# Mixer B's third score product: 128 rows instead of 64

## The chip, the cores and the metric

The kernel runs on one core of a Trainium2 chip. The metric is the device time of one execution in microseconds, the median of several. TensorE multiplies and transposes, VectorE and ScalarE work on tiles in SBUF and PSUM, GpSimd on tiles in SBUF; each takes its instructions in order. TensorE is written PE in the profile, its weight loads PEld, VectorE DVE, ScalarE ACT, GpSimd POOL, SyncE SP.

## The reference

One inference step of four layers over 640 tokens (512 sample tokens, 128 prompt tokens) of 1024 features. Each layer is a token mixer and an MLP with squared ReLU; the mixers go A, B, C, A. All arithmetic is float32. The change concerns mixer B, the second layer, a latent attention with 16 heads:

```python
q = (rmsnorm(h @ w_dq, g_q) @ w_uq).reshape(b, t, N_HEADS, NOPE_DIM + ROPE_DIM)   # 64 + 32
kv = (c_kv @ w_ukv).reshape(b, t, N_HEADS, NOPE_DIM + V_DIM)
k = jnp.concatenate([k_nope, broadcast(k_rope)], axis=-1)      # k_rope: one for all heads
p = softmax(q @ k^T * 96 ** -0.5);  o = p @ v
```

Sample rows see 128 context keys and the 512 sample keys, 640 in all; prompt rows see the 128 prompt keys. So a head has scores of 512 x 640 and of 128 x 128.

## The kernel before

**Two parts.** TensorE gets its operands in the type fp32r, which carries fewer bits than float32. So each operand is split into a high part (ScalarE copies it and rounds) and a low part (VectorE subtracts), and a product is made as high x high + low x high + high x low. In mixer B a query block has 128 rows: the 64 features of the head as high parts and, in the other 64 rows, as low parts. For an even head the high parts are in rows 0 to 63, for an odd one in rows 64 to 127.

**Keys of a pair.** Heads are taken by pairs (class PairB). `nk` (line 729) makes both heads' keys in PSUM, rows 0 to 63 the first head's, rows 64 to 127 the second's, in two parts of 384 columns (t = 0, 1). `ka` (741) copies head e's rows into a tile `kt[e]` of its own as high parts, `kc` (750) copies them again into that tile's other 64 rows, and `kb` (754) writes the low parts into the third tile, `kt[2]`, which both heads share: each has 64 rows of it.

**Scores.** `Kern.qk` (1019) makes a score block with three products: the query block with the doubled high keys (128 rows: high x high and low x high), the rotary query block `R` with `Kr` (128 rows), and the query block's 64 rows of high parts with the low keys (64 rows). `Pair.qk` (407) calls it for a block of 128 sample queries twice, once for each 320 of the 640 keys; `zq` (534) calls it for both heads' prompt queries with 256 columns, the second 128 of which are used. The scores lie in two PSUM tiles of two banks, named psl; `mx` (427, VectorE) copies them out negated with the least value, `ex` (ScalarE) takes exponentials, `sc` (449, GpSimd) scales. Then TensorE transposes the probabilities (`tr`: ps<-cst,p), ScalarE and VectorE split them (ar<-ps) and TensorE multiplies with the values (ps<-ar,VS). Transpositions, projections and keys share three PSUM banks (`tb`).

**Tiles.** High and low parts of weights and keys lie in twelve tiles named wa, each 128 x 1024, a queue: `walloc` (887) takes from its front, `wfree` appends. Twelve are there in all (line 821). The key tiles are given back when the pair's nine score steps are made (`done`, 772); a weight's two tiles when its last product is made.

**Order.** `attend` (1077) goes through the list PLAN["B"] once for each of 8 pairs and their lags; each entry is a step of a pair ("ka00.2": key step of part 0, head 0, of the pair that began two rounds before). The steps' calls are made in exactly this order, so each engine's queue follows it. In a round, eight score steps (64 over the eight pairs) and one prompt step of a pair stand among other steps; behind the last of them come the next pair's projections: `nq`, `nk` on TensorE, `nh`, `ka`, `kc` on ScalarE, `nl`, `kb` on VectorE. Beside the fifth pair and after it, part of the output projection runs too. All engine calls of recorded stages are made at line 283, hence "L283" in the profile.

Of the kernel before, what the change touches and what calls it, by code (L numbers as in the profile page):

```python
# [21 lines left out]
T = 640  # L22
# [22 lines left out]
# the order of the recorded calls of each phase  # L45
# [167 lines left out]
# the steps of two heads (Pair) in the order of a round, each with the rounds that it lags behind its pair's first  # L213
# [33 lines left out]
class Engine:  # L247
    """an engine whose calls go through Calls"""
# [8 lines left out]
class Calls:  # L257
    """the core; between keep and replay the engines' calls are kept, to be made in an order of their own"""
# [26 lines left out]
    def cut(self):  # L285
        """what follows on the tensor engine is no part of the group of products before it"""
        self.apart = True
# [17 lines left out]
class Stream:  # L305
    """Weight units in the order of their use: loaded, and split into two parts that fp32r carries exactly."""
# [44 lines left out]
    def open(self):  # L351
        """past a None, at which fill stops"""
        self.n += 1
# [11 lines left out]
class Pair:  # L365
    """Two heads' attention in steps named as in PLAN: a method and the head, block or group that it takes.

    Sample rows: scores (qk), negated copy and its least value (mx; sk puts the sink beside it), exponentials with
    their sums (ex), inverse sums (rc), scaling (sc), by key blocks transposition (tr), its two parts (hi, lo) and the
    product with the values (pv), at last the output's two parts (oh, ol). The z steps do the same for the prompt rows.  # L370
    """
# [17 lines left out]
    @property  # L389
    def st(self):  # L390
        """[-max | sum | 1/sum] of eight row blocks and the two of the prompt"""
        if self.st_ is None:
            self.st_ = self.k.sts()
        return self.st_
# [28 lines left out]
    def x(self, e, b, sink=0):  # L423
        """the row block's probabilities (sink = 1: with the sink's, which lies before them)"""
        return self.X[e, b // 2][:, b % 2, 1 - sink:1 + A_WIN[b][1]] if self.A else self.X[e, b]
# [78 lines left out]
    def pa(self, e):  # L504
        """stacked products: the values' low parts' beside the high ones'"""
        if e == 0:
            self.o32 = self.k.po.popleft()
        r = 64 * e
        self.nc.scalar.activation(self.o32[r:r + 64, :], self.V[64 - r:128 - r, :], AF.Copy)
# [92 lines left out]
class PairB(Pair):  # L602
    """Mixer B's pair: also its weights (w), queries (n, xf: the last) and keys (k); an even one's, the rotary queries (g)
    and the values (v) of four heads; beside the fifth, the output projection of the first four (y); beside the last,
    weights of the next projection (f)."""
# [135 lines left out]
    def ka(self, t, e):  # L741
        if t + e == 0:
            self.kt = self.k.walloc(3)
            for i in (0, 1):
                self.k.KB[self.hs[i]] = (self.kt[i], self.kt[2])
        r = 64 * e
        ks = slice(t * 384, t * 384 + 384)
        self.nc.scalar.activation(self.kt[e][r:r + 64, ks], self.K[t][r:r + 64, :384], AF.Copy)
# [5 lines left out]
    def kb(self, t, e):  # L754
        r = 64 * e
        ks = slice(t * 384, t * 384 + 384)
        self.nc.vector.tensor_tensor(out=self.kt[2][r:r + 64, ks], in0=self.K[t][r:r + 64, :384], in1=self.kt[e][r:r + 64, ks].bitcast(F32), op=ALU.subtract)
        if e:
            self.k.tb.append(self.K[t])
# [43 lines left out]
class Kern:  # L803
# [19 lines left out]
    def psum(self, pairs):  # L823
        """the lower four banks as two tiles of two banks, or as single ones"""
        if self.psum_cm:
            if bool(self.pairs) == pairs:
                return
            self.psum_cm.close()
        self.psum_cm = ExitStack()
        self.psum_i += 1  # L830
        pool = self.psum_cm.enter_context(self.tc.tile_pool(name=f"psl{self.psum_i}", bufs=1, space=bass.MemoryType.PSUM))
        n = 2 if pairs else 4
        t = [pool.tile([P, 2, 512] if pairs else [P, 512], F32, name=f"psl{self.psum_i}_{i}") for i in range(n)]
        self.pairs = t if pairs else None
        self.all_banks = self.hi_banks if pairs else t + self.hi_banks
        self.banks = self.all_banks
        self.si = 0
# [5 lines left out]
    @contextmanager  # L843
    def ordered(self, n, sync=False):
        """engine calls of a phase, made in ORDER's order at its end"""
        self.nc.phase = n
        self.nc.keep()
        yield
        order = ORDER.get(n) or n[2:] == "attn" and range(len(self.nc.kept))
        E = mybir.EngineType  # L850
        with self.tc.manual_schedule(engines={E.PE, E.DVE, E.Activation, E.Pool} | ({E.SP} if sync else set())) if order else nullcontext():
            self.nc.replay(order)
        self.nc.phase = None

    def open_x(self):
        """what a norm needs, on the other side of SBUF: from one phase's end through the next's first part"""
# [26 lines left out]
    def renew(self, ts, dt):  # L883
        """the same places as new tiles of type dt: what is not rounded to fp32r never lies in a tile that a product reads"""
        return [self.slot(*self.slots.pop(id(t))[1:], dt) for t in ts]
# [15 lines left out]
    def mm_half(self, ps, w, xh, xl, half, nk=8, m=P, wc=P, cut=False, kts=None):  # L901
        """ps[:, :320] += W^T x for one token half; w = (hi, lo) tile of nk blocks."""
# [12 lines left out]
    # ---- residual update and the running sum of squares of the next norm  # L915
# [18 lines left out]
    def newton(self, out, ms, y, t, eng=None):  # L934
        """out = -2 ms^-1/2 from y = exp(-ln(ms)/2)"""
        nc = self.nc
        e = eng or nc.vector
        e.tensor_tensor(out=t, in0=y, in1=ms, op=ALU.mult)
        e.tensor_tensor(out=t, in0=t, in1=y, op=ALU.mult)
        nc.vector.scalar_tensor_tensor(out=out, in0=t, scalar=-3.0, in1=y, op0=ALU.add, op1=ALU.mult)  # L940

    def rstd(self, half, n):
        """1/sqrt(mean of squares + eps) of a token half, on every partition (PSUM)."""
# [18 lines left out]
    def norm(self, half, l, i, r=None):  # L962
        """normalised and modulated input of layer l's mixer (i = 0) or MLP (i = 1)"""
# [28 lines left out]
    # ---- rotary: sample columns turned, prompt columns as they are  # L992
# [5 lines left out]
    def rope_begin(self, src, half, tp, tabs, sh, eng=None, psum=False):  # L998
        """what reads the source, and a function for the rest"""
# [18 lines left out]
    # ---- attention, by head: scores and softmax (s1), transposed probabilities times V (s2)  # L1018
    def qk(self, o, h, E, R, bs, ks):
# [5 lines left out]
        else:  # L1025
            kh, klp = self.KB[h]
            r = 64 * (h % 2)
            nc.tensor.matmul(o, E[:, bs], kh[:, ks], start=True, stop=False)
            nc.tensor.matmul(o, R[:, bs], self.Kr[:, ks], start=False, stop=False)
            nc.tensor.matmul(o, E[r:r + 64, bs], klp[r:r + 64, ks], start=False, stop=True)  # L1030

    def group(self, h):
        """key head of the query head at place h (HEADS)"""
        return 2 * (h // 8) + h % 2

    def v_parts(self, h, kb, th, tl):
        """the products that make a head's output of a value block: (values, probabilities)

        stacked: a block's two heads as [high | low | low | high], so that one product gives both parts' sums in two
        halves of the rows; else [high | zeros | high] and the same of the low parts, the other head's rows left as they are  # L1040
        """
# [20 lines left out]
    def v_put(self, kb, src):  # L1062
        """values of four heads: key block kb < 5, or the prompt's own"""
# [3 lines left out]
    def v_place(self, kb, src):  # L1067
        """places of the high and the low parts, and the source in their shape"""
# [8 lines left out]
    def attend(self, Q, O):  # L1077
        """every pair's steps, each at its place in time"""
# [14 lines left out]
    # ---- mixers A and C  # L1093
    def mixer_ac(self, l):
# [6 lines left out]
        with ExitStack() as lc:  # L1101
# [14 lines left out]
            with tc.tile_pool(name=f"qkv{l}", bufs=2) as tp:  # L1116
# [17 lines left out]
                def rotated(ps, g, half):  # L1134
                    """the rotated rows, in mixer C normalised by head before: begun in steps, then (tile, end)"""
# [136 lines left out]
    # ---- mixer B  # L1272
# [98 lines left out]
    # ---- MLP  # L1371
# [10 lines left out]
    def run_units(self, n, xh, xl, evac, ret_first=0, ret_last=None, step=None, nk=8, drain=True, ready=None):  # L1382
        """n units over both token halves; at the start ret_first units' first halves go before their second, at the end RET units' if ret_last"""
# [34 lines left out]
    def advance(self):  # L1418
        """the pending evacuations' next stages, the latest's first"""
# [6 lines left out]
    def mlp(self, l, oproj):  # L1426
        """the mixer's output projection, and the MLP"""
# [52 lines left out]
    # ---- modulation: six parts of [128, 2, 8], the scales with one and the norm's gain in them  # L1480
# [6 lines left out]
    def mod_done(self, l, k, n=0, src=None):  # L1487
        """the bias, and a scale's gain; the first n columns come from src"""
# [13 lines left out]
    def ada_tile(self, l, k, i, mix=False, dma=None):  # L1502
        """mod k's f tile i: silu(c) . w_ada[:, f], per partition"""
# [29 lines left out]
    def start(self):  # L1533
        """the first layer's first two modulations, on every engine at once, and its first norm"""
# [122 lines left out]
def rope_tables(hd, gw, rep):  # L1657
    """cos and signed sin, [2, 128, 512]: rows of each head: two halves (grid row, grid column) of gw features"""
# [99 lines left out]
```

## Time and profile before

| | |
|---|---|
| runs | 3161.24, 3162.58, 3162.84 us; median 3162.58 |
| profiled execution | span 3157.8 us, first to last instruction; its own time is given by no other figure |
| runs less that span | 3.4 to 5.0 us |
| TensorE / its weight loads | 3028.6 us (96%) / 2916.5 us (92%) |
| VectorE, ScalarE, GpSimd | 2236.3 (71%), 1374.9 (44%), 655.0 us (21%) |
| granted TensorE clock | 0.984 of full over the span; 1.00 in mixer B's attention |
| mixer B's attention | about 893 to 1180 us of the span |

The page of the profile lists the busy time of each engine; windows cut it into stretches; waits say who waited for whom; a timeline shows instructions in order, equal ones merged. A matmul's length in the rows goes from its start to the modelled end of its pipeline, so products overlap: what one costs is seen from start to start.

### The profile page before, as it was taken

To read this page: it belongs to the slowest core of one execution; us is meant where nothing else is said; L and a number is where in the kernel's file an instruction comes from. 1 tells how busy PE (TensorE), PEld (TensorE's weight loads), DVE (VectorE), ACT (ScalarE), POOL (GpSimd) and SP (SyncE) were. 2 spreads that over 40 slices of the span, in tenths; PEclk is the share of its full clock that TensorE was granted. 3 is DMA by queue.
4 is the path that set the end of the run, shared out by engine and by line. 5 is a ranking of instruction groups with operands and counts; after the bars stand their busy time and mean duration, and the time that the engine had idled before them with its cause. 6 is when DMAs were issued, how large, how long until landed. Compare 5 with 4: busy or idle time off the path is not lost. (4 is left out here: it accounts for less than half of the span.)

```text
span 3157.8 us, 52023 instructions
## 1 busy us (share of the span) xinstructions
PE 3028.6 (96%) x20016; PEld 2916.5 (92%) x20016; DVE 2236.3 (71%) x4697; ACT 1374.9 (44%) x2895; POOL 655.0 (21%) x744
## 2 busy tenths in 40 slices
PE   6789899999999999999999899999999999999998
PEld 6789899999978879999998789999999899999998
DVE  8998977676677678777648897766755896633434
ACT  3577423223467565223236795422323484422321
POOL 4556420000033233000002473000000261000000
PEclk8799999999999999999999999999999999999999
DMA  6302344443111114444321103344422101222221
GB/s 217 106 24 89 126 165 147 149 150 125 50 35 46 36 37 163 147 150 150 121 77 36 44 1 128 113 148 148 151 96 84 44 1 64 91 74 74 79 76 47
DMA packets 89305, 300.84 MB, mean 95 GB/s; under 512 B 11104, under 2 KB 15920, under 8 KB 88672
## 3 DMA queue, kind: packets, MB, share of 16 engines
q1 hardware_dynamic: 64816, 210.35, 20.2%
q0 software_dynamic: 24240, 87.16, 8.4%
q8 instruction: 157, 2.57, 0.3%
q14 instruction: 92, 0.75, 0.1%
HBM read 288.66 MB, written 3.56 MB: 93 GB/s over the span
## 5 line engine op out<-in xcount | busy, mean ns | idle before, releaser
L283 PE MATMUL ps<-ar,wa 128*128 128x320 f32 x6752 | 1149.3, 311 | 21.6 <-DVE ar L283 15.0
L283 PE MATMUL psl<-ar,wa 128*128 128x320 f32 x6392 | 1087.6, 311 | 11.3 <-ACT ar L283 3.7
L283 PEld LDWEIGHTS ps<-ar,wa 128*128 128x128 f32 x6752 | 1035.0, 189 | 30.5 <-DVE ar L283 20.2
L283 PEld LDWEIGHTS psl<-ar,wa 128*128 128x128 f32 x6392 | 981.6, 189 | 14.1 <-ACT ar L283 4.1
L283 ACT ACTIVATE wa<-wraw 128x1024 fp32r<-128x1024 f32 (+3 forms) x350 | 360.0, 1030 | 935.2 <-PE psl L283 433.8
L283 DVE TENSOR_TENSOR wa<-wraw,wa 128x1024 fp32r<-128x1024 f32 (+2 forms) x336 | 410.5, 1222 | 277.2 <-ACT wa L283 274.6
L283 DVE CUSTOM_DVE_ANT_0 junk<-adaw,cb 128x1024 bf16<-128x1024 f32 x333 | 419.8, 1261 | 11.0 <-DMA adaw<-ada 10.3
L283 PE MATMUL ps<-ex,wa 128*128 128x320 f32 x1312 | 324.0, 316 | 15.3 <-ACT rpq L283 8.8
L283 PE MATMUL psl<-ex,wa 128*128 128x320 f32 x1312 | 321.5, 314 | 5.7 <-DVE wa L283 3.3
L283 POOL TENSOR_TENSOR p<-p,st 128x640 f32<-128x640 f32 (+2 forms) x256 | 277.1, 1104 | 220.7 <-DVE st L283 162.0
L283 PE MATMUL psl<-wa,ar 128*128 128x320 f32 (+5 forms) x1040 | 271.2, 356 | 18.2 <-DVE wa L283 4.5
L283 POOL DMA_DIRECT2D adaw<-ada x152 | 81.1, 534 | 944.6 <-DVE mod L283 929.6
L283 PEld LDWEIGHTS ps<-ex,wa 128*128 128x128 f32 x1312 | 230.2, 191 | 19.1 <-ACT rpq L283 9.0
L283 ACT ACTIVATE ar<-ps 128x512 fp32r<-128x512 f32 (+5 forms) x452 | 208.1, 490 | 89.4 <-PE ps L283 83.0
L283 DVE TENSOR_TENSOR ar<-ps,ar 128x512 fp32r<-128x512 f32 (+3 forms) x416 | 224.1, 561 | 28.8 <-ACT ar L283 25.7
L283 PEld LDWEIGHTS psl<-ex,wa 128*128 128x128 f32 x1312 | 228.4, 190 | 8.6 <-DVE wa L283 4.2
L283 PEld LDWEIGHTS psl<-wa,ar 128*128 128x128 f32 (+1 forms) x1040 | 171.8, 194 | 69.8 <-issue 38.3
L283 DVE SCALAR_TENSOR_TENSOR x<-ps,mod,x 128x320 f32<-128x320 f32 (+2 forms) x264 | 107.4, 435 | 181.1 <-PE ps L283 181.0
L283 DVE SCALAR_TENSOR_TENSOR x<-psl,mod,x 128x320 f32<-128x320 f32 (+2 forms) x240 | 98.4, 435 | 189.4 <-PE psl L283 189.4
L283 ACT ACTIVATE p<-p,st 128x640 f32<-128x640 f32 (+2 forms) x256 | 190.6, 748 | 19.1 <-DVE st L283 8.8
L283 PE MATMUL ps<-cst,p 128*128 128x128 f32 x1088 | 155.3, 275 | 4.0 <-DVE wa L283 2.7
L283 DVE TENSOR_TENSOR usq<-relu 128x320 f32<-128x320 f32 x256 | 128.6, 504 | 40.3 <-ACT relu L283 38.2
(205 smaller groups left out, 3038.9 us busy)
## 6 DMA issues: line engine op xcount, KB each, us to landing
adaw<-ada POOLq DMA_DIRECT2D x152, 512.0 KB, 4.6
wraw<-win SPq DMA_DIRECT2D x128, 512.0 KB, 3.4
wraw<-wout SPq DMA_DIRECT2D x128, 512.0 KB, 3.5
wraw<-qkv SPq DMA_DIRECT2D x36, 512.0 KB, 3.5
wraw<-wo SPq DMA_DIRECT2D x24, 512.0 KB, 3.5
adaw<-ada SPq DMA_DIRECT2D x23, 512.0 KB, 7.0
wa<-ada SPq DMA_DIRECT2D x13, 512.0 KB, 3.5
ar<-wa SPq DMA_DIRECT2D x64, 80.0 KB, 2.1
```

Of the source, the lines that this page charges most:

```text
L283: return m(*a, **k)
```

## The change

The pair takes four wa tiles instead of three. Each head gets a low-key tile of its own, `kt[2 + e]`: its low parts are in the same 64 rows as before, and GpSimd sets the other 64 rows to zero over all 768 columns, in the pair's first key step (two memsets a pair, sixteen in all). The third score product then takes all 128 rows of the query block, the same block as the first product, and of that tile: the rows of low query parts meet zeros. The diff also takes out comments and docstrings, which give no instruction.

```diff
     def ka(self, t, e):
         if t + e == 0:
-            self.kt = self.k.walloc(3)
+            self.kt = self.k.walloc(4)
             for i in (0, 1):
-                self.k.KB[self.hs[i]] = (self.kt[i], self.kt[2])
+                self.k.KB[self.hs[i]] = (self.kt[i], self.kt[2 + i])
+                self.nc.gpsimd.memset(self.kt[2 + i][64 - 64 * i:128 - 64 * i, :768].bitcast(F32), 0.0)
...
     def kb(self, t, e):
-        self.nc.vector.tensor_tensor(out=self.kt[2][r:r + 64, ks], in0=self.K[t][r:r + 64, :384], in1=self.kt[e][r:r + 64, ks].bitcast(F32), op=ALU.subtract)
+        self.nc.vector.tensor_tensor(out=self.kt[2 + e][r:r + 64, ks], in0=self.K[t][r:r + 64, :384], in1=self.kt[e][r:r + 64, ks].bitcast(F32), op=ALU.subtract)
...
     def qk(self, o, h, E, R, bs, ks):
-            kh, klp = self.KB[h]
-            r = 64 * (h % 2)
+            kh, kl = self.KB[h]
             nc.tensor.matmul(o, E[:, bs], kh[:, ks], start=True, stop=False)
             nc.tensor.matmul(o, R[:, bs], self.Kr[:, ks], start=False, stop=False)
-            nc.tensor.matmul(o, E[r:r + 64, bs], klp[r:r + 64, ks], start=False, stop=True)
+            nc.tensor.matmul(o, E[:, bs], kl[:, ks], start=False, stop=True)
```

## Rows read from the trace of the kernel before

**Rows 1.** The page, busy us and share of each engine.
```profile
PE 3028.6 (96%) x20016; PEld 2916.5 (92%) x20016; DVE 2236.3 (71%) x4697; ACT 1374.9 (44%) x2895; POOL 655.0 (21%) x744
```

**Rows 2.** Waits, 885 to 1190 us: waiter, releaser: total us, times, longest.
```profile
PEld psl L283 <- issue: 34.6, 193, 0.2
DVE ar L283 <- ACT ar L283: 26.8, 51, 1.3
DVE p L283 <- PE psl L283: 21.0, 35, 1.3
...
PEld ps L283 <- DVE wa L283: 6.5, 7, 1.7
PEld ps L283 <- issue: 6.5, 41, 0.2
```

**Rows 3.** Windows: stretch, length; busy (instructions) by engine; clock; DMA.
```profile
893.00:1180.00 287.00, 282.45 (x1710) 231.32 (x1710) 206.60 (x490) 188.64 (x441) 98.46 (x85) 1.00 0.14 38
```

**Rows 4.** Groups by form, 885 to 1190: busy, mean ns, idle before.
```profile
L283 PE MATMUL psl<-wa,ar 64*128 64x320 f32 x128 | 52.5, 410 | 0.0
...
L283 PE MATMUL psl<-Kr,ar 128*128 128x320 f32 x128 | 39.3, 307 | 0.0
...
L283 PEld LDWEIGHTS psl<-wa,ar 64*128 64x128 f32 x144 | 26.3, 183 | 26.6 <-issue 24.4
```

**Rows 5.** Timeline, TensorE, 988 to 1028: start, length, operation, count.
```profile
990.86 0.39 PE L283 MATMUL psl<-wa,ar 128*128 128x320 f32 x1
...
992.49 0.44 PE L283 MATMUL ps<-cst,p 128*128 128x128 f32 x2
...
1004.72 0.28 PE L283 MATMUL psl<-wa,ar 128*128 128x256 f32 x1
...
1006.11 1.09 PE L283 MATMUL ps<-cst,p 128*128 128x128 f32 x8
...
1012.04 0.31 PE L283 MATMUL psl<-wa,ar 128*128 128x320 f32 x1
...
1013.60 1.58 PE L283 MATMUL ps<-ar,wa 128*128 128x320 f32 x9
...
1018.45 1.81 PE L283 MATMUL ps<-ar,VS 128*128 128x256 f32 x14
1020.09 1.48 PE L283 MATMUL ps<-ar,wa 128*128 128x320 f32 x9
```

**Rows 6.** Windows, layer 0's MLP.
```profile
600.00:800.00 200.00, 200.00 (x1366) 200.00 (x1365) 137.42 (x247) 61.41 (x101) 12.73 (x24) 1.00 0.41 133
```

**Rows 7.** Windows, the dense stretches of pairs 1, 2, 4 and 7.
```profile
924.09:947.24 23.15, 23.15 (x128) 17.04 (x128) 18.28 (x47) 16.43 (x40) 10.31 (x10) 1.00 0.07 21
...
956.31:981.76 25.45, 25.45 (x150) 19.35 (x150) 18.39 (x49) 16.61 (x41) 9.50 (x9) 1.00 0.19 53
...
1022.66:1049.83 27.17, 27.17 (x160) 21.07 (x161) 20.44 (x52) 18.24 (x45) 11.28 (x10) 1.00 0.18 48
...
1149.43:1171.20 21.77, 21.77 (x120) 15.69 (x120) 15.60 (x41) 14.57 (x36) 9.51 (x9) 1.00 0.00 1
```

**Rows 8.** Windows, layer 0's attention.
```profile
200.00:220.00 20.00, 20.00 (x136) 18.43 (x135) 19.35 (x63) 19.22 (x57) 15.72 (x29) 1.00 0.00 1
```

**Rows 9.** Groups by form, GpSimd, whole span.
```profile
L283 POOL TENSOR_TENSOR p<-p,st 128x640 f32<-128x640 f32 x128 | 160.1, 1274 | 189.0 <-DVE st L283 143.0 <-PE psl L283 41.6 <-PE ps L283 4.2
...
L283 POOL MEMSET VH<- 128x640 f32 x2 | 1.3, 632 | 79.1 <-DVE ar L283 75.7 <-ACT adaw L283 3.4
```

**Rows 10.** Timeline, GpSimd, 978 to 992.
```profile
983.98 0.88 POOL L283 TENSOR_TENSOR rps<-rps,tabb 128x320 f32<-128x320 f32 x1
990.73 2.47 POOL L283 TENSOR_TENSOR p<-p,st 128x640 f32<-128x640 f32 x2 [5.87 <-DVE st L283]
```

**Rows 11.** Timeline, VectorE, 978 to 992.
```profile
986.48 1.14 DVE L283 TENSOR_TENSOR wa<-ps,wa 64x384 fp32r<-64x384 f32 x2 [0.62 <-ACT wa L283]
```

**Rows 12.** Timeline, ScalarE, 1058 to 1066.
```profile
1063.55 0.63 ACT L283 ACTIVATE wa<-wraw 128x512 fp32r<-128x512 f32 x1 [3.82 <-DMA wraw<-wo]
```

## The prediction

> **What bounds the kernel now.** I read the page's busy line first: TensorE holds 96% of the span, its weight loads 92%, VectorE 71% [rows 1]. Then I cut out the stage that the change touches, mixer B's attention. Its 287.00 us, from the first score product to the last pair's scores, show TensorE busy for 282.45 us, VectorE for 206.60, ScalarE for 188.64 and GpSimd for 98.46 [rows 3]. So TensorE sets the length there, and the other engines follow.
>
> The waits of this stage tell what TensorE waits for. Its weight loads lose 34.6 us ahead of score products and 6.5 us ahead of others to "issue", that is, to nothing that another engine owes; 6.5 us go to VectorE's writes into wa tiles [rows 2]. VectorE for its part waits 21.0 us for score products and 26.8 us for ScalarE's high parts [rows 2]. The by-form groups put the "issue" in one place: the 144 weight loads of 64 rows have 26.6 us of idle time before them, 24.4 of it "issue", and the 64x320 products read 410 ns where the 128-row Kr products beside them read 307 [rows 4].
>
> A read-out of 307 ns overlaps the next product, so a price has to come from start to start. A score group is six products: three for each half of the keys, the third of 64 rows. One group begins at 990.86 and the next product at 992.49: 1.63 us. Another, which follows products with values, takes 1012.04 to 1013.60: 1.56 us. The prompt's group, 256 columns wide, takes 1004.72 to 1006.11: 1.39 us [rows 5]. Where all products have 128 rows and 320 columns, 1366 of them fill 200 us, 0.146 us each [rows 6]; at 256 columns fourteen take 1018.45 to 1020.09, 0.117 each [rows 5]. Six full-height products would take 0.88 and 0.70 us.
>
> **The third product.** No product is added or removed: 8 pairs x 2 heads x 4 row blocks = 64 groups, and 8 prompt groups. If a 128-row third product runs at the pitch of its neighbours, a sample group falls by 1.56 - 0.88 = 0.68 us, or by 1.63 - 0.88 = 0.75 us where the longer start of a group belongs to the change of height too. A prompt group falls by 1.39 - 0.70 = 0.69. Together 64 x 0.68 + 8 x 0.69 = 49.0 us, and 53.5 with 0.75. I take 49.0, since the longer start occurs behind transposes, which stay. The "issue" waits alone, 41.1 us [rows 2], are an independent reading from the other side. Two ends for this edit: nothing (height has no price), and 53.5.
>
> A page speaks against it. The Trainium skill, in "TensorE: Matmul & The Clock Gate", section "Why this matters for your kernels", says that a single product with a small contraction takes the same time as one of 128 rows; by this alone the gain would be nil. "TensorEngine Tiling (Array Packing)", section "Key Properties", says that a change of tiling mode drains TensorE; by this the whole 49 us are to be had. The rows above side with the second: the extra time lies around the 64-row products, before and behind them.
>
> **What VectorE and ScalarE leave of it.** Each pair's eight groups and its prompt group lie in one dense stretch, and lose 8 x 0.68 + 0.69 = 6.1 us there. The stretch behind it (projections of the next pair's queries and keys) has no score product and keeps its length. What is late next in the dense stretch is VectorE, which copies and reduces the scores and makes the low parts. New TensorE time against VectorE's work [rows 7]: pair 1, 23.15 - 6.1 = 17.05 against 18.28, and pair 3 has the same pattern; pair 2, 19.35 against 18.39; pair 4, 21.07 against 20.44; pair 7, 15.67 against 15.60. The other three have more room. So in pairs 1 and 3 VectorE becomes the bound, and what counts is how full its queue can be in a fixed order. Today pair 1 has it at 79%, but behind TensorE. Layer 0's attention, the same steps in an order of its own, keeps it at 19.35 us of 20 [rows 8], 97%, with ScalarE nearly as full at 19.22. At 97% the stretches lose 1.8 us in pairs 1 and 3 and 0.4 in pair 7: 4.0 us. At 85%, back towards today's rate, pairs 1 and 3 lose 4.45 each, pair 2 2.3, pair 4 3.0 and pair 7 2.7: 17 us. I take 93%, nearer to the row that shows an order under this load: 19.66 - 17.05 = 2.6 in pairs 1 and 3, 0.4 in pair 2, 0.9 in pair 4, 1.1 in pair 7, about 8 us in all. Kept: 49 - 8 = 41 us.
>
> **The zeros.** Sixteen memsets of 64 x 768 go to GpSimd, two in each pair's first key step. The nearest row, a memset of 640 columns, takes 632 ns; by columns one of these takes 0.76 us. The dearest neighbour is the scaling, 1274 ns for 640 columns, 1.53 us by columns; the low end is nothing [rows 9]. I take 0.76: 12 us of GpSimd's 98 in 287. They run behind two scalings and the rotary product, which in pair 3's key step end at 983.98 + 0.88 = 984.86 [rows 10]; so they end at 986.4. The first that could need them is VectorE's low part of the keys, at 986.48 [rows 11], a margin of 0.1 us; queued behind them on GpSimd is only the scaling of 990.73, which waits for VectorE anyway [rows 10]. Even pairs' key steps have no rotary product ahead of them on GpSimd. I cost them at nothing; without that cover they cost up to 2 x 0.76 us a pair, 12 us.
>
> **The fourth tile.** walloc takes 4 of 12 wa tiles instead of 3. Counting walloc and wfree along the plan, the free list reaches 0 in several places but never goes below it. A high part now and then takes a tile that was freed more lately: a unit of output-projection weights beside pair 5 takes the tile that a product freed three steps before. ScalarE waited 3.82 us for their DMA there [rows 12], so this costs nothing. The key tiles that wait for the last pair's scores are written behind this pair's key products, which TensorE makes later than those scores. No DMA is added or moved past another.
>
> **The sum.** -49 + 8 + 0 + 0 = -41 us. The profiled span is 3157.8 us; the runs shown lie 3.4 to 5.0 us above it, the median 4.8. So 3116.8 + 4.8, rounded to 3122 us.
>
> **The rivals.**
> *The whole relief.* VectorE keeps pace at 97% or better, and the longer starts go too: a gain of 45 to 54 us, 3109 to 3117 us. For it: layer 0's row [rows 8], and that VectorE's own waits are for TensorE. Against: mixer B's order was laid for score groups of 1.6 us.
> *VectorE takes the place.* Its waits for ScalarE's high parts stay, TensorE waits for a transposition bank or a score tile instead of for the drain, in every pair: a gain of 6 to 28 us (85% would still give 49 - 17 = 32), 3134 to 3156 us. For it: pair 1's sum of 17.05 against 18.28, and ScalarE close behind; against: five of eight pairs have room.
> *Height has no price.* The stall belongs to the third product for another reason, such as the same stationary block being loaded again: 3160 to 3169 us. Against: the 64-row loads alone have the idle time, the equal blocks' first loads do not.
> *Slower: the memsets gate the low keys.* If the low parts wait for both memsets of the tile, and these wait for late scalings, the pair's key banks come free late and TensorE stands at the next transposition, where it waits for wa writes today [rows 2]. Price: at most 2 x 1.53 us and one pair of scalings, 2 x 1.27, some 5.6 us a pair, 45 us in eight. It decides when it exceeds the relief that is left: above 41 / 8 = 5.1 us a pair; at 5.6 the time would be 3166, and with half the relief gone to VectorE 3187. It needs every pair to be late by the whole of it; the margins above speak against it.
>
> **How the numbers follow.** Forecast (gain 28 to 45 us) 0.46, whole relief 0.25, VectorE takes the place 0.19, no price 0.06, slower 0.04. Of these, the first three are faster; a measurement can tell about 0.2%, 6.3 us, from no change. Faster 0.90, same 0.06, slower 0.04. The range 3107 to 3148 us leaves out the worst third of the VectorE case and the two cases behind it, and a little below.
>
> **What would show it.** In the profile after: no 64-row form; score groups of six at 0.9 to 1.0 us; the "issue" wait ahead of score products gone. VectorE at 90% or more in pairs 1 and 3, and TensorE's new idle time there named as VectorE's. Sixteen memsets near 0.76 us that nobody waits for. Wrong would be: groups still at 1.4 us or more; or a TensorE wait of several us in each pair, on VectorE's wa writes or on GpSimd.

## The result and the profile after

The changed kernel takes 3113.43 us, the median of four runs (3111.24 to 3116.19), where the kernel before takes 3162.02 in the runs beside it (3161.24 to 3162.84). The ratio is 0.9844, its 95% interval 0.983 to 0.9858: 48.6 us less. The prediction said 3122 with a range of 3107 to 3148, and "faster" at 0.90. Direction, place and mechanism came out as told. The size did not: the forecast's own case was a gain of 28 to 45 us, and 48.6 lies in the case beside it, called "the whole relief" (3109 to 3117).

The page after, busy line and span (answers to [rows 1]): TensorE is busy 47 us less, in a span that is 46.6 us shorter than 3157.8; its weight loads are busy as long as before.

```profile
span 3111.2 us, 52045 instructions
PE 2981.5 (96%) x20016; PEld 2916.1 (94%) x20016; DVE 2232.6 (72%) x4697; ACT 1373.2 (44%) x2895; POOL 668.0 (21%) x760
```

The windows of mixer B's attention say where the time went. I cut both kernels at the same instructions: from the first nine products for pair 0 behind the keys' products, to the first product of the output projection behind the last pair. Before, the stage and pair 2 in it (columns as in [rows 3]):

```profile
956.31:990.45 34.14, 33.49 (x206) 27.15 (x206) 24.39 (x61) 23.85 (x57) 12.60 (x11) 1.00 0.15 40
...
893.24:1181.99 288.75, 283.06 (x1712) 231.62 (x1712) 207.81 (x493) 190.16 (x444) 99.05 (x86) 1.00 0.14 38
```

After, the eight pairs, the stage, and pair 1's dense stretch with the stretch behind it:

```profile
892.95:918.46 25.51, 23.80 (x173) 23.13 (x174) 20.68 (x53) 19.86 (x49) 10.29 (x10) 1.00 0.28 74
918.46:944.99 26.53, 25.37 (x188) 24.86 (x188) 25.02 (x60) 24.08 (x57) 14.03 (x13) 1.00 0.17 43
944.99:972.41 27.42, 26.80 (x205) 26.43 (x205) 23.93 (x61) 23.44 (x57) 14.04 (x13) 1.00 0.19 49
972.41:999.15 26.74, 25.34 (x187) 24.83 (x187) 25.01 (x60) 24.14 (x57) 14.06 (x13) 1.00 0.17 45
999.15:1040.43 41.28, 40.56 (x298) 40.17 (x299) 33.24 (x78) 26.60 (x63) 17.41 (x15) 1.00 0.20 59
1040.43:1078.45 38.02, 37.79 (x277) 37.48 (x275) 30.53 (x72) 24.66 (x57) 13.37 (x13) 1.00 0.14 39
1078.45:1106.27 27.82, 27.20 (x212) 26.84 (x209) 22.94 (x57) 23.23 (x56) 11.94 (x11) 1.00 0.18 46
1106.27:1133.35 27.08, 24.00 (x180) 22.39 (x180) 22.55 (x57) 22.38 (x53) 14.78 (x13) 1.00 0.04 11
892.95:1133.35 240.40, 230.87 (x1712) 226.14 (x1712) 203.91 (x493) 188.40 (x444) 109.91 (x100) 1.00 0.17 46
918.46:936.04 17.58, 16.82 (x129) 16.55 (x130) 17.32 (x43) 15.58 (x39) 10.08 (x9) 1.00 0.10 27
936.04:944.99 8.95, 8.55 (x62) 8.31 (x60) 7.70 (x18) 8.50 (x20) 3.94 (x4) 1.00 0.31 74
```

The stage falls from 288.75 to 240.40 us, by 48.35; all the rest together is 1.7 us longer (46.6 - 48.35), for a reason that no run isolates. Cut at the same instructions, the pairs before lasted 30.85, 32.22, 34.14, 32.21, 47.86, 44.43, 34.48 and 32.56 us. So they gain 5.34, 5.69, 6.72, 5.47, 6.58, 6.41, 6.66 and 5.48. Four of them (2, 4, 5, 6) gain 6.4 to 6.7, the others 5.3 to 5.7.

The groups by form (answers to [rows 4]) have no 64-row form left, and no "issue" wait before score products. The third products have joined the first ones' form, x256 at 325 ns. GpSimd has sixteen memsets more:

```profile
L283 PE MATMUL psl<-wa,ar 128*128 128x320 f32 x256 | 70.6, 325 | 2.8 <-DVE st L283 2.8
L283 PEld LDWEIGHTS psl<-wa,ar 128*128 128x128 f32 x288 | 51.0, 188 | 3.7 <-DVE st L283 3.6
L283 PE MATMUL psl<-Kr,ar 128*128 128x320 f32 x128 | 39.8, 311 | 0.0
...
L283 POOL MEMSET wa<- 64x768 f32 x16 | 11.8, 735 | 1.9 <-PE ps L283 0.8 <-POOL p L283 0.3
```

TensorE's timeline (answers to [rows 5]) shows a score group of six products, and below it the place of a new wait:

```profile
918.88 0.39 PE L283 MATMUL psl<-wa,ar 128*128 128x320 f32 x1
919.11 0.31 PE L283 MATMUL psl<-Kr,ar 128*128 128x320 f32 x1
919.25 0.45 PE L283 MATMUL psl<-wa,ar 128*128 128x320 f32 x2
919.54 0.31 PE L283 MATMUL psl<-Kr,ar 128*128 128x320 f32 x1
919.68 0.31 PE L283 MATMUL psl<-wa,ar 128*128 128x320 f32 x1
919.84 0.38 PE L283 MATMUL ps<-cst,p 128*128 128x128 f32 x2
...
931.45 0.38 PE L283 MATMUL ps<-cst,p 128*128 128x128 f32 x2
932.59 0.41 PE L283 MATMUL psl<-wa,ar 128*128 128x320 f32 x1 [0.76 <-DVE st L283]
...
989.32 0.31 PE L283 MATMUL psl<-wa,ar 128*128 128x320 f32 x1
...
990.20 1.48 PE L283 MATMUL ps<-ar,wa 128*128 128x320 f32 x9
```

From 918.88 to 919.84 a group that follows transpositions lasts 0.96 us, where it was 1.63. From 989.32 to 990.20 one that follows products with values lasts 0.88, where it was 1.56 (1012.04 to 1013.60 in [rows 5]). The operation behind a group got shorter as well: nine products behind one read 1.58 [rows 5] and now 1.48.

The waits after, 885 to 1145 us (answers to [rows 2]):

```profile
DVE ar L283 <- ACT ar L283: 6.7, 15, 1.1
PEld ps L283 <- DVE wa L283: 6.5, 7, 1.7
...
PE ps L283 <- DVE wa L283: 4.8, 7, 1.4
...
PE psl L283 <- DVE st L283: 2.8, 3, 1.1
...
DVE p L283 <- PE psl L283: 2.0, 8, 0.5
```

VectorE waits far less for these two: 21.0 to 2.0 us for score products, 26.8 to 6.7 for high parts. TensorE's wait for wa writes is the old one. New is "PE psl <- DVE st", three times: a score group waits for a score tile that VectorE has not yet copied out.

### The profile page after: what moved, and what is told of

It is laid out like the page before. It is cut to its first block, busy times and chain, and to the rows that moved or that the text cites. A ratio compares the mean times of both kernels' runs of the same rounds, so it can differ in the third digit from the quotient of the medians.

```text
span 3111.2 us, 52045 instructions
## 1 busy us (share of the span) xinstructions
PE 2981.5 (96%) x20016; PEld 2916.1 (94%) x20016; DVE 2232.6 (72%) x4697; ACT 1373.2 (44%) x2895; POOL 668.0 (21%) x760
## 5 line engine op out<-in xcount | busy, mean ns | idle before, releaser
L283 PE MATMUL psl<-wa,ar 128*128 128x320 f32 (+3 forms) x1040 | 240.1, 335 | 20.9 <-DVE st L283 5.7
L283 ACT ACTIVATE ar<-ps 128x512 fp32r<-128x512 f32 (+5 forms) x452 | 208.0, 490 | 52.4 <-PE ps L283 48.6
L283 PEld LDWEIGHTS psl<-wa,ar 128*128 128x128 f32 x1040 | 169.5, 195 | 35.5 <-DVE st L283 14.5
```

The lines of the kernel that those rows point to most:

```text
L283: return m(*a, **k)
```

## The experiments

Three questions were open: whether height is the whole cause and where its price lies; whether the zeros cost anything; and what the three new waits are worth. e1 to e4 share a chip and 17 runs of the kernel before (3160.57 us), e5 to e8 another (9 runs, 3160.66), e9 and e10 a third (9 runs, 3163.46). Beside each median stands the length of the attention stage in the profiled execution, cut as above. Three profiles of the changed kernel or of one that issues the same TensorE work (after, e7, e8) give 240.40, 240.85 and 240.87, so a stage is read to about 0.5 us.

**e1, the tiles without the height.** The changed kernel, third product on 64 rows again.

```diff
-            nc.tensor.matmul(o, E[:, bs], kl[:, ks], start=False, stop=True)
+            r = 64 * (h % 2)
+            nc.tensor.matmul(o, E[r:r + 64, bs], kl[r:r + 64, ks], start=False, stop=True)
```

> The changed kernel with its four tiles and sixteen memsets, but the third score product on 64 rows again. Theory (the height of the third product is the whole gain): about 3162 us, within 6 of the kernel before; the 144 weight loads of 64 rows have about 25 us of issue waits before them again, a sample group takes 1.56 to 1.63 us from start to start, and the memsets (0.73 us each) cost nothing. Rival (a part of the gain comes from the low keys having a tile of their own, or from another order of tile reuse): clearly below 3156 us.

Measured: 3161.88 us (10 runs), ratio 1.0004 [0.9994, 1.0013], stage 289.10. The groups by form bring the stall back as it was in [rows 4]:

```profile
L283 PE MATMUL psl<-wa,ar 64*128 64x320 f32 x128 | 52.5, 410 | 0.0
...
L283 PEld LDWEIGHTS psl<-wa,ar 64*128 64x128 f32 x144 | 26.3, 183 | 26.6 <-issue 24.4
```

Four tiles and sixteen memsets alone neither gain nor cost anything that the runs can tell: the stage is within 0.35 us of the kernel before (288.75).

**e2, the height without the tiles.** The kernel before, three tiles, no memset, third product over all rows of the shared tile.

```diff
-            nc.tensor.matmul(o, E[r:r + 64, bs], klp[r:r + 64, ks], start=False, stop=True)
+            nc.tensor.matmul(o, E[:, bs], klp[:, ks], start=False, stop=True)
```

> The kernel before with one edit: the third score product takes all 128 rows of the query block and of the shared low-key tile. There are no memsets and three tiles, so the scores also get the low query parts times the other head's low keys, which the reference does not have. Theory (height alone): 3113 us within 4, a sample group at 0.88 to 0.97 us. Rival (memsets or the fourth tile cost or save something beside it): off by more than 5 us from the changed kernel's 3113.

Measured: 3113.44 us, ratio 0.9846 [0.9832, 0.9861], stage 240.11. A group lasts 0.97 us (955.56 to 956.53). With e1 this is the full separation: the height is the whole gain, as far as the runs can tell.

**e3, two 64-row products side by side.** The kernel before; in a sample group the two third products are made last, behind the other four.

```diff
-            for i in (0, 1):
-                k.qk(..., slice(i * HT, i * HT + HT))
+            for part in (0, 1) if self.B else (None,):
+                for i in (0, 1):
+                    k.qk(..., slice(i * HT, i * HT + HT), part)
```

Part 0 makes the first and the rotary product, part 1 the third.

> The kernel before, in each sample score group the two 64-row products at the end, one behind the other (first, rotary, first, rotary, third, third); prompt groups as they were. As many 64-row products, half as many changes of height. Theory (the price is paid at a change of height between neighbours): a group loses half of its extra 0.75 us, 64 x 0.37 = 24 us, so about 3138 us. Rival (the price belongs to each 64-row product): 3162 us within 6. Second rival (the price belongs to the same query block being loaded again one product later, in the row of third and next first): gone altogether or nearly, 3113 to 3120.

Measured: 3139.6 us, ratio 0.9928 [0.9913, 0.9943], stage 265.37, 23.4 less than before (the medians differ by 21.0). Timeline of one group, TensorE:

```profile
955.50 0.39 PE L283 MATMUL psl<-wa,ar 128*128 128x320 f32 x1
955.73 0.31 PE L283 MATMUL psl<-Kr,ar 128*128 128x320 f32 x1
955.88 0.31 PE L283 MATMUL psl<-wa,ar 128*128 128x320 f32 x1
956.02 0.31 PE L283 MATMUL psl<-Kr,ar 128*128 128x320 f32 x1
956.26 0.56 PE L283 MATMUL psl<-wa,ar 64*128 64x320 f32 x2
956.75 0.74 PE L283 MATMUL ps<-ar,VS 128*128 128x256 f32 x4
```

The group lasts 1.25 us with the same six products. The rotary product takes 0.24 to the next start instead of 0.15; the second 64-row product follows the first by 0.15 (0.56 less 0.41, the length of a single one). So the price belongs to the change of height, not to a 64-row product as such: half the changes cost about half of it (23.4 of the 48.35 us are saved).

**e4, the rotary product on 64 rows too.** The kernel before; the number of changes of height stays.

```diff
-            nc.tensor.matmul(o, R[:, bs], self.Kr[:, ks], start=False, stop=False)
+            nc.tensor.matmul(o, R[r:r + 64, bs], self.Kr[r:r + 64, ks], start=False, stop=False)
```

> The kernel before with the rotary product also on 64 rows, those of the third product (the other 64 rows of it are left out, so the scores lack a part). Twice as many 64-row products, as many changes of height. Theory (price at a change of height): 3162 us within 8, the pair of 64-row products at 0.15 to 0.2 us from start to start. Rival (price for each 64-row product): another 48 to 54 us, about 3213 us.

Measured: 3169.14 us (8 runs, 3159.61 to 3174.57), ratio 1.0028 [1.0018, 1.0039], 8.6 us more than the 3160.57 beside it: inside the 3162 within 8 that was expected, near its end, and far from the 3213 of a price per 64-row product. A group lasts 1.65 us (955.11 to 956.76). The groups by form show the stall moved to the first 64-row load of a run, and gone from the second:

```profile
L283 PEld LDWEIGHTS psl<-wa,ar 64*128 64x128 f32 x144 | 27.1, 188 | 0.0
L283 PEld LDWEIGHTS psl<-Kr,ar 64*128 64x128 f32 x144 | 26.5, 184 | 22.5 <-issue 20.4
```

Its stage lasts 291.89 us, 3.1 more than before. The rest of the 8.6 isn't in the profiled execution, which at 3159.61 is the shortest of the eight; the others had granted clocks of 0.978 to 0.982 over the span, those of the kernel before 0.979 to 0.984. Whether that explains it stays open.

**e7 and e8, each memset twice, and the changed kernel again.**

```diff
-                self.nc.gpsimd.memset(self.kt[2 + i][...].bitcast(F32), 0.0)
+                for _ in (0, 1):
+                    self.nc.gpsimd.memset(self.kt[2 + i][...].bitcast(F32), 0.0)
```

> The changed kernel with each of the sixteen memsets made twice, 32 in all, 0.73 us each. Theory (nobody waits for them): 3113 us within 3, as the changed kernel. Rival (they gate the low keys or hold up the scalings behind them): 1.5 us a pair, 12 us in all, 3125 us.

> The changed kernel once more, as the partner of the three runs beside it: 3113 us within 3; TensorE's waits in mixer B's attention again at three score groups for a score tile that VectorE frees (1.1, 0.8 and 1.0 us, pairs 0, 1 and 3) and seven times for a bank that VectorE's low keys free (4.8 us).

Measured: e7 3113.63 us, ratio 0.9851 [0.9838, 0.9865]; e8 3114.03, ratio 0.9851 [0.9838, 0.9865]. In e8 TensorE's waits come back as expected: three for a score tile (2.9 us in all) and seven for wa writes (4.7 us). GpSimd's timeline in e7, in pair 1's first key step:

```profile
915.74 0.88 POOL L283 TENSOR_TENSOR rps<-rps,tabb 128x320 f32<-128x320 f32 x1
916.68 3.10 POOL L283 MEMSET wa<- 64x768 f32 x4
921.70 2.46 POOL L283 TENSOR_TENSOR p<-p,st 128x640 f32<-128x640 f32 x2 [1.91 <-DVE st L283]
```

Even four memsets leave 1.91 us of idle time before the next scaling. VectorE's two low parts run beside them, from 917.51 to 918.64: they begin 0.03 us after the last of ScalarE's four copies (917.48), not after the memsets (919.78). The prediction had named these low parts as the first that could need the zeros; they do not wait for them. The zeros are free in time.

**e5 and e10, VectorE's rotary addition later.** In the timeline of VectorE in the changed kernel, ahead of the wait at 932.59:

```profile
930.78 1.21 DVE L283 TENSOR_TENSOR rpq<-rpq,rps 128x192 f32<-128x192 f32 x1
932.02 0.29 DVE L283 CUSTOM_DVE_ANT_0 z<-psl,zero 128x128 f32<-128x128 f32 x1
...
932.24 0.29 DVE L283 CUSTOM_DVE_ANT_0 z<-psl,zero 128x128 f32<-128x128 f32 x1
932.45 0.08 DVE L283 DVE_READ_ACCUMULATOR2_ANT st<- 128x1 f32 x1
```

The two copies (z<-psl) free the score tile; the addition (`ga1`), 1.21 us long, stands in front of them. These two kernels, equal to each other, put it behind them in the order list:

```diff
-... ex11.3 ga1.2 zq.3 zm0.3 zm1.3 ...
+... ex11.3 zq.3 zm0.3 zm1.3 ga1.2 ...
```

> The changed kernel with one step moved in the order of a round: the second half's rotary addition on VectorE (1.2 us) comes behind the two copies of the prompt's scores, not ahead of them. Theory (where the relief fell short in pairs 1 and 3, TensorE waited for a score tile behind this addition): the waits of 0.76 and 0.98 us there are gone or under 0.2, pairs 1 and 3 last about 25.7 us where they lasted 26.5 and 26.7, the whole some 1.7 us less, too little for the time to tell. Rival (VectorE is simply full there): the waits move on to another place, and the pairs last as before.

> The changed kernel with the rotary addition later, once more, as the partner of the run beside it: 3110 us within 3.

Measured: 3110.31 us, ratio 0.9842 [0.9829, 0.9855], stage 238.45; again 3110.33, ratio 0.984 [0.9826, 0.9853], stage 238.38. The wait is left once instead of three times, the same row in both:

```profile
PE psl L283 <- DVE st L283: 1.1, 1, 1.1
```

Pairs 1 and 3 get 0.71 and 0.69 us shorter (25.82 and 26.05 in e10). The stage is 2 to 2.5 us shorter, twice, beyond the 0.5 of reading. The medians are 3.7 us (e5 beside e8) and some 3 us (e10, on another chip) below the changed kernel, but their intervals overlap with its: I can't call this version faster, only its stage shorter.

**e6, the copies of the keys in another order.** e5, and ScalarE's doubling copy (`kc`) of a key part behind both first copies (`ka`), so that VectorE's low keys could begin earlier.

```diff
-... nk0.2 ka00.2 kc00.2 ka01.2 kc01.2 kb00.2 ...
+... nk0.2 ka00.2 ka01.2 kc00.2 kc01.2 kb00.2 ...
-... ka11.2 nl11.2 kc11.2 ka10.2 kc10.2 kb10.2 kb11.2 ...
+... ka11.2 nl11.2 ka10.2 kc11.2 kc10.2 kb10.2 kb11.2 ...
```

> The same with a second edit of the order: in the key steps ScalarE makes both heads' first copies before the doubled ones, so that VectorE's low keys can begin one copy (0.49 us) earlier. Theory: VectorE's waits of about 0.6 us ahead of the second pair of low keys fall to 0.1 to 0.2, TensorE's seven waits for that bank (0.4 to 0.6 us each) fall below 0.2 each: 3 us more, some 5 us below the changed kernel, 3108 us. Rival (ScalarE's total work there sets the time, or the next step behind is late instead): under 1 us beside the run with one edit.

Measured: 3111.48 us, ratio 0.9844 [0.9831, 0.9858], stage 239.07; TensorE's wait for wa writes still 4.7 us. The theory fell. The low keys still began only when the fourth copy had ended: ScalarE's four run from 943.78 for 1.96 us to 945.74, VectorE's pair begins at 945.78.

**e9, the doubling copy out of the tile.** e6, with `kc` reading the high part from SBUF instead of the same PSUM bank.

```diff
-        self.nc.scalar.activation(self.kt[e][64 - r:128 - r, ...], self.K[t][r:r + 64, :384], AF.Copy)
+        self.nc.scalar.activation(self.kt[e][64 - r:128 - r, ks], self.kt[e][r:r + 64, ks].bitcast(F32), AF.Copy)
```

> The run with both orders, and with the doubled high keys copied by ScalarE from the rounded ones in the tile, no longer from the PSUM bank: the bank then has one copy of each head and one subtraction to wait for. Theory (the low keys waited for all four copies because these read the same bank): VectorE's second pair of low keys begins behind the second copy, about 1 us earlier; TensorE's seven waits for that bank (0.4 to 0.6 us, 4.7 in all) fall below 0.2 each, some 3 us less, 3107 us beside 3110. Rival (ScalarE's four copies have to be made anyway, and the doubled ones are needed first): the waits stay or move to the first score group of the pair, 3110 us.

Measured: 3111.56 us, ratio 0.9838 [0.9824, 0.9851], stage 236.39, 2.0 less than e10. Waits of the stage, TensorE:

```profile
PE ps L283 <- DVE ar L283: 3.4, 9, 1.3
PE ps L283 <- DVE wa L283: 1.4, 1, 1.4
...
PE psl L283 <- DVE st L283: 0.7, 1, 0.7
```

The wait for wa writes falls from 4.6 us in seven places (e10) to 1.4 in one, so it hung on ScalarE's copies out of the keys' bank, which VectorE's subtraction from the same bank had followed; here a pair of low parts begins at 946.10, while ScalarE's doubling copies last until 946.59. Whether the bank or the order that the program keeps between its readers made it follow was not separated. A third of the wait comes back as waits for ar (2.4 to 3.4). The expected 3107 was not met, though the stage is shorter: the profiled execution begins it 3.5 us later than e10's (897.14 against 893.64). A wait "<-DVE rpq" ahead of it does not explain this: it is 2.37 us in e9 (886.75) and 2.89 in e10 (883.21). 2.5 of the 3.5 us are there before 876 us already, and why stays open. The other 1.0 falls together with a lower clock. From 879 us on, behind the same waits as in e10 (0.30 and 0.54 us), TensorE starts products of 320 columns 0.26 us apart in e9, 0.15 in e10. The granted clock from 880 to 885 us reads 0.73 of full, so a part of that stretch ran at the lower of its two levels, 1.2 and 2.4 GHz; e10's reads 1.00 at these products. Why it fell stays open.

## Why the prediction was right, and where a term was off

**The bound and the place** held. TensorE's stall around 64-row products was the cost, in this stage alone, and e1, e2 and e3 isolate it. "TensorEngine Tiling (Array Packing)", section "Key Properties", of the Trainium skill says that a change of tiling mode drains TensorE; e3's 1.25 and e4's 1.65 us agree. "TensorE: Matmul & The Clock Gate", section "Why this matters for your kernels", of the Trainium skill says that a single product with a small contraction takes the time of a 128-row one; that holds for e3's second neighbour (0.15 us) and not across a change.

**The third product.** I took 0.68 us a group, since I put the longer start of some groups down to the transposes. That was right: groups behind transposes fell from 1.63 to 0.96 us, others from 1.56 to 0.88, 0.67 and 0.68, and the longer start stays. What I left out is the operation behind a group: it had paid for the change back (nine products 1.58, now 1.48), and a price read from a group's first start to the next operation's misses that. With it pairs 2 and 6 gain 6.72 and 6.66, so an estimate for eight pairs is 53.5 us. My upper end was 53.5 too, 8 x (8 x 0.75 + 0.69), but by luck: its reason, that the longer start goes, did not come true. This term was 4.5 us too small.

**What VectorE leaves of it.** Predicted 8 us, measured 53.5 - 48.35, about 5, and not all of it VectorE's. This is the other mis-sized term, by 3 us, in the same direction. It failed in three ways. I took the dense stretch as closed and VectorE at 93% in it: by the rows it went to 17.32 of 17.58 us in pair 1, 98.5%, and four instructions slid behind the boundary (43 there, 47 in [rows 7]), into a stretch that had room. So pairs 1 and 3 lost 1.0 and 1.2 us instead of 2.6, and pair 4 next to nothing instead of 0.9. About 0.85 of those 17.32 us VectorE spent held up by GpSimd (last section); without them it is 93.7%, so which share was the better guide, the 97% of layer 0 [rows 8] or my 93%, stays open. And pair 0, which I gave room, lost 1.35: its third group waits 1.09 us at 897.56 for the first score copy, which VectorE begins only at 896.68, behind a shuffle and a rotary product. Pair 7 lost 1.2 where I had 1.1, by luck: its dense stretch (1106.27 to 1121.66) lasts 15.39 where it was 21.76, a relief of 6.37. Three quarters of its loss, 0.9 us, lie behind that stretch, and most of them in one wait of TensorE for GpSimd's scaling, before and after:

```profile
1173.51 1.31 PE L283 MATMUL ps<-cst,p 128*128 128x128 f32 x10 [0.17 <-POOL p L283]
...
1124.87 1.31 PE L283 MATMUL ps<-cst,p 128*128 128x128 f32 x10 [0.72 <-POOL p L283]
```

**The zeros**: 0.735 us each for 0.76, and nothing on the path, shown by e7. **The fourth tile**: nothing, shown by e1.

**The sum.** -53.5 + 5.2 = -48.3 where -41 was told, and 1.7 us given back elsewhere in the profiled execution. The 4.8 us that I added to the span is no distance between span and time: in every later run that lists both, the time is 1.7 to 1.9 us above the span. So the span of 3157.8 belongs to an execution of about 3159.6 us (an estimate), faster than the median; that is why the medians differ by 48.6 us and the spans by 46.6. The rivals: "height has no price" fell with e1 and e2, the slower one with e7. "VectorE takes the place" is true of three waits and 2.8 us. "The whole relief" has the size, without one of its two reasons: the longer starts stayed.

## What to carry to other kernels

Price a stall from start to start over a whole repeated unit, with the first operation behind it included; the idle time in the profile names the cause but splits the price over two neighbours. When a resource becomes the bound in a stretch, ask what can slide over the stretch's end before giving time back for it. And where products of different heights alternate on TensorE, either make them equal with zero rows or put the short ones side by side: the first saved 48 us of this stage, the second 23.

## What the runs showed of the hardware that was not expected

*The length of VectorE's addition is GpSimd's.* The rotary addition of 192 columns reads 0.36 to 1.21 us for the same work. In pairs 1, 3 and 5 it reads 0.69 to 1.21 and ends 0.20 to 0.22 us after scalings that GpSimd had begun before it: in the kernel before, in the changed one and in e5 to e10. In GpSimd's timeline of the changed kernel, beside the row at 930.78 above:

```profile
929.31 2.47 POOL L283 TENSOR_TENSOR p<-p,st 128x640 f32<-128x640 f32 x2
```

The scalings end at 931.78, the addition at 931.99. In pair 3 it is 985.98 and 986.19, in e5 931.34 and 931.55, in e10 932.43 and 932.64, in the kernel before 940.88 and 941.09. Ahead of pair 0 no scaling runs, and the same addition reads 0.36 us: in the kernel before (889.09) with GpSimd idle, in the changed one while the two memsets run:

```profile
888.41 1.52 POOL L283 MEMSET wa<- 64x768 f32 x2
888.81 0.36 DVE L283 TENSOR_TENSOR rpq<-rpq,rps 128x192 f32<-128x192 f32 x1 [0.46 <-DVE rpq L283]
```

So the addition was held until the scalings were done, for about 0.85 of its 1.21 us in pair 1 (an estimate, 1.21 - 0.36), and in pairs 1 and 3 the chain of the new wait is scaling, addition, copies, score group. The Trainium skill, "SBUF — State Buffer", section "Who interferes with whom", says that a VectorE instruction with two SBUF inputs contends with a GpSimd instruction that reads SBUF; these ends agree, and so does the 0.36 beside memsets, which read nothing. No run took the scaling away from pair 1, so it is read from rows and not tested by an edit.

*A busy share can contain such holding.* In pair 1 VectorE reads 98.5% busy for 17.6 us, with ScalarE at 89% beside it and TensorE losing 0.76 us; less the 0.85 us it is 93.7%.
